# A two-block transformer: the first loads in another order, x's first chunk ahead of the first weight splits, and buffers in multiples of 32 columns

## The chip, the core and the metric

The kernel runs on one core of a Trainium2 chip. The core has a matrix engine (TensorE, PE in the profile), a vector engine (VectorE, DVE), a scalar engine for functions by table (ScalarE, ACT), a general engine (GpSimd, POOL) and an engine that only issues transfers (SyncE, SP). ScalarE and GpSimd can issue transfers too, and 16 DMA engines carry them out. The metric is the time of one execution on the device in microseconds (us), as the median of several runs.

## The reference

Two transformer blocks follow each other on one sequence of 256 tokens of width 2048, all in float32. The weights are drawn at random; the large ones are read once each.

```
h = layer_norm(a*x + hybrid_mixer(x))          # block 1
h = layer_norm(a*h + memory_cross_attention(h, mem))
h = layer_norm(a*h + conv_ffn(h))
for layer in (0, 1):                           # block 2
    n = rmsnorm(h)
    h = h + (even_mixer(n) if layer == 0 else short_conv(n))
    h = h + mlp(rmsnorm(h))                    # relu squared, 2048 -> 8192 -> 2048
```

The hybrid mixer multiplies x by one wide matrix `w_in` and cuts the product into pieces for three mixers, whose outputs stand side by side before `w_out`:

- S5: a diagonal complex recurrence along the tokens. Its coefficients come from small tables (exponential, cosine, sine and a division of the parameters), and the recurrence is a scan.
- Stick-breaking attention (SB): 8 heads of 64 with a running sum of logarithms in place of the softmax.
- Sparse attention (NSA): 16 heads of 64 with a compressed branch, a selected branch and a window. For the compressed branch, blocks of 32 keys (and values) get a position added and go through a small two-layer network, whose first weights are `nsa_cmp_w1`.

The even mixer of block 2 has attention heads with low-rank keys and values and an average over windows of tokens.

## The kernel before, in words

**Weights.** Nearly all the time is products of 256 tokens with large weights. The weights come in chunks of 1 MB (512 rows by 512 columns) on SyncE's queue (`load`, L628) into a ring of three buffers `raw`. Each float32 product is made of three products of a faster number type: a chunk is split into a high part `whi`, made by ScalarE (`split_hi`, L645), and the rest `wlo`, made by VectorE (`split_lo`, L655), each in two halves of 128 x 1024 and in rings of four. The activations are split likewise into slots `rt`. One half is used by four weight groups of TensorE: two matmuls of 512 columns and two of 256, or three of 512. A chunk's buffer is free again when its second half is split, and a half's when TensorE has used it.

**Order.** Nothing is reordered on the chip: each engine works through a list that is fixed when the program is built, and semaphores hold an instruction until its operands are there. The list is written by a planner, the `Builder`. It walks through the weight groups one by one. Beside them it has "side threads", generators that issue everything else in small steps: the transposes of x, S5's set-up and its chunks, the heads of the attentions, the sums of the compressed branch. After each group `advance` (L509) takes steps from the side threads as long as its own clocks of the engines allow. These clocks are estimates: `spent` (L438) adds one for each instruction, and `region` (L423) remembers, for each stretch of 32 columns of a buffer, when it was last written and last read. `wait_for` (L544) takes steps until something that is needed is there. The space for buffers is given out by an `Arena`; among the holes that are large enough it prefers one whose stretches are free soonest (`late`, L123). A step of a thread is thus put elsewhere when an estimate, the size of a buffer or its place changes.

**Start.** `network` (L2939 to L2963) issues the first loads: `load_consts` (L800) the constants `cbig` (128 x 1004, with the unit matrix `ident` in its first 128 columns) on ScalarE's queue; then, for each of four chunks c, `stage` (L2526) a quarter of x (512 KB; the first on SyncE's queue, the other three on ScalarE's) and, for the first three, a weight chunk on SyncE's queue. At c = 2 GpSimd makes a copy of one column that reads x's third chunk; GpSimd's own loads, some 20 small ones, stand behind it. `s5.load`, `nsa.load` and `load_cols` (L819) issue the small parameters. `run` (L752) first splits two halves (`ahead(2)`, L755), then goes through the plan; at the start of the first entry `start` (L2564) queues the side threads: S5's set-up and, for each chunk of x, `trans` (L2531), which transposes four pieces of 128 columns on TensorE, two matmuls each, and splits them into `rt`.

**Places the rows speak of.** h0 and h1 are the first products of the compressed branch, for keys and for values: 16 matmuls of 128 x 60 each, written by `hid_part` (L2604), which read `nsa_cmp_w1` from `raw` and the blocks that `NSA.gather` (L2287) has collected and added the positions to (an addition of 128 x 960). S5's set-up (`S5.setup`, L1895) runs on GpSimd, VectorE, ScalarE and, with small matmuls of 33 rows, on TensorE; `S5.chunk` (L2060) is one piece of the scan. Nearly every instruction has the line of the recording helper, L233, so rows are told apart by operation and buffers: `ft` is the space for float32 buffers, `st` a small one, `bank` a bank of the matmul's accumulators.

## Time and profile before

| | |
|---|---|
| median of 3 runs | 3513.49 us (3511.28 to 3513.76) |
| the profiled execution | 3515.05 us |
| its span in the trace | 3513.3 us, so 1.75 us lie around it |
| mean granted clock of TensorE | 0.989 of full speed |
| TensorE busy | 3426.3 us, 98% of the span |
| VectorE busy | 2371.4 us, 67% |
| ScalarE busy | 1725.5 us, 49% |
| GpSimd busy | 215.7 us, 6% |
| moved by the DMA engines | 605.15 MB, 172 GB/s on the mean |

A row of the timeline gives the start and the duration of an instruction, or of several alike that follow each other (x and a count), and in brackets how long the engine stood idle before it and what ended that. Float32 matmuls and matmuls of two passes appear as two records each. A row of a table of stretches gives, for each engine, its busy time and in parentheses its number of records. The granted clock is the share of full speed that the chip allows TensorE: 1.00 is 2.4 GHz and 0.50 is 1.2 GHz; a figure in between is a mean over a stretch. The chain that ended last is TensorE's work for 87% of the span and VectorE's for 10%.

### The profile page before, as it was taken

What the parts mean: (1) busy time and instruction counts of PE and PEld (TensorE: products, weight loads), DVE (VectorE), ACT (ScalarE), POOL (GpSimd) and SP (SyncE); (2) the same over time, 40 slices, a digit from 0 to 9 for tenths busy, and PEclk for the clock granted to TensorE, in tenths of its full rate; (3) what the DMA queues carried; (4) which work ended last, traced back from release to release, by engine and by line L of the source; (5) the groups of instructions that cost most, each with busy time, mean ns of one, the idle gap of its engine ahead of it and who ended that gap; (6) DMA issues with size and microseconds to landing.
All of it is one profiled execution on the core that took longest, in us unless ns stands there. A gap on an engine that the chain in (4) does not pass through costs nothing.

```text
span 3513.3 us, 49562 instructions
## 1 busy us (share of the span) xinstructions
PE 3426.3 (98%) x19448; PEld 2940.8 (84%) x19448; DVE 2371.4 (67%) x3978; ACT 1725.5 (49%) x2652; POOL 215.7 (6%) x319
## 2 busy tenths in 40 slices
PE   8998999899999999999999999999999999999999
PEld 6777688788888887787888888888888888888887
DVE  4977677876676578877765656567666664656565
ACT  4445645555455455654544444444454544434343
POOL 4001010001000001000000000000221000000001
PEclk8999999999999999999999999999999999999999
DMA  5452244355555555443555555555555555555554
GB/s 181 132 166 96 56 168 165 134 192 188 187 191 192 187 186 167 150 126 126 170 190 192 188 186 189 192 180 192 184 189 191 192 191 186 187 191 192 186 187 143
DMA packets 323779, 605.15 MB, mean 172 GB/s; under 512 B 18843, under 2 KB 36243, under 8 KB 323545
## 3 DMA queue, kind: packets, MB, share of 16 engines
q1 hardware_dynamic: 319609, 596.91, 51.5%
q10 hardware_dynamic: 3264, 4.19, 0.5%
q8 instruction: 152, 2.49, 0.3%
q0 software_dynamic: 672, 0.89, 0.1%
q14 instruction: 82, 0.67, 0.1%
HBM read 599.26 MB, written 2.69 MB: 171 GB/s over the span
## 4 chain that ended last, share of the span: by engine, by line
PE 87%; DVE 10%; issue 1%; ACT 1%; POOL 1%; DMA 1%; ACTq 0%; SPq 0%; DVEq 0%; POOLq 0%
PE bank L233 87%; DVE ft L233 6%; DVE wlo L233 3%; POOL ft L233 1%; DVE rt L233 0%; ACT ft L233 0%; DMA ft<-in_x_dram 0%; ACT whi L233 0%; DMA raw<-in_w_in_dram 0%; DMA raw<-in_even_w_ukv_dram 0%; DMA raw<-in_even_w_uq_dram 0%; POOL st L233 0%; DVE st L233 0%; ACT rt L233 0%; ACT L284 0%
## 5 line engine op out<-in xcount | busy, mean ns | idle before, releaser
L233 PE MATMUL bank<-rt,whi 128*128 128x512 f32 (+1 forms) x8784 | 2785.7, 399 | 47.6 <-DVE ft L233 27.3
L233 PEld LDWEIGHTS bank<-rt,wlo 128*128 128x128 f32 (+1 forms) x8784 | 1651.7, 189 | 388.8 <-DVE wlo L233 0.4
L233 DVE TENSOR_TENSOR wlo<-raw,whi 128x1024 fp32r<-128x1024 f32 x1134 | 1379.2, 1222 | 719.6 <-ACT whi L233 717.1
L233 ACT ACTIVATE whi<-raw 128x1024 fp32r<-128x1024 f32 x1134 | 1189.4, 1050 | 1344.3 <-PE bank L233 1271.5
L233 PE MATMUL bank<-rt,wlo 128*128 128x256 f32 (+1 forms) x8784 | 1727.8, 279 | 0.0
L233 PEld LDWEIGHTS bank<-rt,whi 128*128 128x128 f32 (+1 forms) x8784 | 1347.6, 189 | 79.6 <-DVE ft L233 28.9
L233 DVE TENSOR_TENSOR ft<-bank,ft 128x256 f32<-128x256 f32 (+2 forms) x879 | 358.3, 420 | 286.7 <-ACT ft L233 198.5
L233 POOL TENSOR_TENSOR ft<-ft 128x256 f32<-128x256 f32 (+1 forms) x179 | 149.1, 844 | 2912.8 <-DVE ft L233 2061.4
L233 ACT ACTIVATE ft<-bank 128x256 f32<-128x256 f32 (+3 forms) x499 | 190.4, 392 | 189.7 <-PE bank L233 161.1
L233 PE MATMUL bank<-ft 128*128 128x128 f32 (+9 forms) x1073 | 213.5, 346 | 33.9 <-DVE ft L233 21.8
L233 DVE SCALAR_TENSOR_TENSOR ft<-ft 128x256 f32<-128x256 f32 (+2 forms) x441 | 225.8, 513 | 13.0 <-ACT ft L233 2.5
L233 PEld LDWEIGHTS bank<-ft 128*128 128x128 f32 (+4 forms) x1073 | 137.6, 171 | 87.6 <-DVE ft L233 25.4
L233 ACT ACTIVATE ft<-ft 128x256 f32<-128x256 f32 (+3 forms) x365 | 165.8, 467 | 90.4 <-DVE ft L233 70.1
L233 DVE TENSOR_TENSOR ft<-ft 128x256 f32<-128x256 f32 (+4 forms) x463 | 194.1, 442 | 14.1 <-ACT ft L233 8.7
L233 ACT ACTIVATE rt<-ft 128x256 fp32r<-128x256 f32 x317 | 138.6, 439 | 85.2 <-DVE ft L233 80.3
L233 DVE TENSOR_TENSOR rt<-ft,rt 128x256 fp32r<-128x256 f32 x220 | 91.7, 445 | 5.2 <-ACT rt L233 5.2
L233 PE MATMUL bank<-whi,rt 128*128 128x256 f32 (+1 forms) x320 | 80.6, 329 | 1.4 <-DVE ft L233 1.4
L233 ACT ACTIVATE ft<-ft,st 128x256 f32<-128x256 f32 (+1 forms) x146 | 64.5, 464 | 19.3 <-DVE st L233 18.5
L233 PEld LDWEIGHTS bank<-whi,rt 128*128 128x128 f32 x320 | 55.5, 190 | 7.6 <-ACT whi L233 1.2
L233 PE MATMUL bank<-wlo,rt 128*128 128x256 f32 (+1 forms) x160 | 52.1, 326 | 0.0
L233 DVE SCALAR_TENSOR_TENSOR rt<-ft,rt 128x256 fp32r<-128x256 f32 x97 | 45.1, 475 | 0.3 <-ACT rt L233 0.3
L233 ACT ACTIVATE rt<-bank 128x256 fp32r<-128x256 f32 x56 | 20.0, 380 | 45.0 <-PE bank L233 44.9
(76 smaller groups left out, 464.9 us busy)
## 6 DMA issues: line engine op xcount, KB each, us to landing
raw<-in_w_mlp_up_dram SPq DMA_DIRECT2D x128, 1024.0 KB, 5.3
raw<-in_w_mlp_down_dram SPq DMA_DIRECT2D x128, 1024.0 KB, 5.1
raw<-in_ffn_w_up_dram SPq DMA_DIRECT2D x88, 1024.0 KB, 5.0
raw<-in_odd_w_in_dram SPq DMA_DIRECT2D x48, 1024.0 KB, 5.2
raw<-in_ffn_w_down_dram SPq DMA_DIRECT2D x44, 1024.0 KB, 5.1
raw<-in_w_in_dram SPq DMA_DIRECT2D x36, 1024.0 KB, 5.1
raw<-in_w_out_dram SPq DMA_DIRECT2D x16, 1024.0 KB, 5.1
raw<-in_even_w_in_dram SPq DMA_DIRECT2D x16, 1024.0 KB, 5.4
```

The lines of the kernel that those rows point to most:

```text
L233: return f(*a, **kw)
```

## The change

Four things are changed. The call that splits the first two halves moves from `run` into `start`, behind the whole transposition of x's first chunk (`now` runs a side thread to its end); the other three chunks of x are side threads as before. Only the 128 columns of the unit matrix are loaded first on ScalarE's queue; the other 876 columns of `cbig` come on SyncE's queue behind the third weight chunk. All of x comes on SyncE's queue, so that this queue has, in order: x's first chunk, a weight chunk, x's second, a weight chunk, x's third, a weight chunk, the rest of `cbig`, x's last chunk, then the small parameters. And three buffers are rounded up: `cbig` from 1004 to 1024 columns, the parameter columns from 584 to 608, the buffer of GpSimd's copy from 1 to 32. With that every buffer in `ft` begins at a multiple of 32 columns.

```diff
--- before.py
+++ after.py
@@ -752,7 +752,6 @@
     def run(self):
         self.halves = [(i, j) for i, e in enumerate(self.plan) for j in range(e.nhalf)]
         self.nhi = self.nlo = self.nhalf = 0
-        self.ahead(2)
         for i, e in enumerate(self.plan):
             for f in e.before:
                 f()
@@ -799,8 +798,9 @@
 
     def load_consts(self):
         nc = self.nc
-        self.cb = self.buf(CBIG.shape[1], True)
-        nc.scalar.dma_start(out=self.cb.ap, in_=self.I["cbig"])
+        self.cb = self.buf(1024, True)
+
+        nc.scalar.dma_start(out=self.cb.ap[:, 0:128], in_=self.I["cbig"][:, 0:128])
         nc.vector.tensor_copy(out=self.identr, in_=self.cst("ident"))
         self.ones = self.buf(128, True)
         nc.vector.memset(self.ones.ap, 1.0)
@@ -819,7 +819,7 @@
     def load_cols(self):
 
         nc = self.nc
-        self.pcol = self.buf(NCOL, True)
+        self.pcol = self.buf((NCOL + 31) // 32 * 32, True)
         nt = (NCOL + 127) // 128
         st = self.buf(nt * 128)
         sv = st.v(nt)
@@ -2525,7 +2525,7 @@
 
     def stage(n, c):
         stg[n, c] = B.buf(1024)
-        (nc.scalar if n == "x" and c else nc.sync).dma_start(out=stg[n, c].v(2), in_=I[n][0, :, c * 512:(c + 1) * 512].rearrange("(t p) f -> p t f", p=128))
+        nc.sync.dma_start(out=stg[n, c].v(2), in_=I[n][0, :, c * 512:(c + 1) * 512].rearrange("(t p) f -> p t f", p=128))
         return stg[n, c]
 
     def trans(n, c, lin=False):
@@ -2562,8 +2562,10 @@
     RT = 0.9
 
     def start():
+        now(trans("x", 0))
+        B.ahead(2)
         B.side(s5.setup())
-        for c in range(4):
+        for c in range(1, 4):
             B.side(trans("x", c), B.ready(stg["x", c].ap))
         B.side(B.turn_cols(), 40000.0)
         B.side(nsa.setup(), 45000.0)
@@ -2950,9 +2952,10 @@
         if c < B.NRAW:
             B.load(c)
         if c == 2:
-
-            t = B.buf(1)
-            nc.gpsimd.tensor_copy(out=t.ap, in_=x.ap[:, 0:1])
+            nc.sync.dma_start(out=B.cb.ap[:, 128:CBIG.shape[1]], in_=I["cbig"][:, 128:])
+
+            t = B.buf(32)
+            nc.gpsimd.tensor_copy(out=t.ap[:, 0:1], in_=x.ap[:, 0:1])
     s5.load()
     nsa.load()
     B.load_cols()
```

The planner's list differs from the first instructions on. The number of instructions hardly does: TensorE has 18896 in both, VectorE 3982 for 3980, ScalarE 2582 for 2586 with 25 loads of function tables for 22 (five scalings went from ScalarE to VectorE), GpSimd 326 for 324. Three places show how the order changes.

The first is TensorE's list at its beginning: before it was this, with transposes of x (`bank<-ft`, 128x128, two to a piece), the transpose of a small 48-row buffer, and the groups of the first weight chunk (`whi0`, `whi1`, and `wlo` of the same number); semaphores with DMAHW stand for loads.

```order
L233 MATMUL bank4_84<-ft_78 128x128 [waits DMAHW1_49,DMAHW0_49]
...
L233 MATMUL bank5_85<-ft_78 128x128 [waits DMAHW2_49]
...
L233 MATMUL bank6_86<-ft_78 128x48 [waits DMASW1_49,DMASW0_49,DVE_49]
L233 MATMUL bank7_87<-ft_78 128x128 x2
L233 MATMUL bank4_84<-ft_78 128x128 [waits DVE_49]
...
L233 MATMUL bank5_85<-ft_78 128x128 [waits DMAHW4_49,DVE_49]
...
L233 MATMUL bank3_83<-rt_76,whi0_68 128x512 [waits Activation_49]
L233 MATMUL bank3_83<-rt_76,whi0_68 128x512 [waits DVE_49]
L233 MATMUL bank3_83<-rt_76,wlo0_72 128x256 x2
...
L233 MATMUL bank7_87<-ft_78 128x128 [waits DMAHW5_49]
...
L233 MATMUL bank2_82<-rt_76,whi0_68 128x512 x2
...
L233 MATMUL bank3_83<-rt_76,whi1_69 128x512 [waits Activation_49]
```

Now the list begins like this:

```order
L233 MATMUL bank4_84<-ft_78 128x128 [waits DMAHW1_49,DMAHW0_49]
...
L233 MATMUL bank5_85<-ft_78 128x128 x2
L233 MATMUL bank6_86<-ft_78 128x128 x2
L233 MATMUL bank7_87<-ft_78 128x128 x2
L233 MATMUL bank3_83<-rt_76,whi0_68 128x512 [waits DVE_49,Activation_49]
L233 MATMUL bank3_83<-rt_76,whi0_68 128x512 [waits DVE_49]
...
L233 MATMUL bank2_82<-rt_76,whi0_68 128x512 x2
...
L233 MATMUL bank3_83<-rt_76,whi1_69 128x512 [waits Activation_49]
...
L233 MATMUL bank4_84<-ft_78 128x128 [waits DMAHW3_49]
...
L233 MATMUL bank5_85<-ft_78 128x128 [waits DMAHW5_49]
...
L233 MATMUL bank7_87<-ft_78 128x128 [waits DMAHW0_49]
...
L233 MATMUL bank3_83<-rt_76,whi2_70 128x512 [waits Activation_49]
```

x's first chunk is transposed whole, all eight groups of the first weight chunk follow, and only then come x's second, third and last chunk (the waits for DMAHW3, DMAHW5 and DMAHW0) and the first group of the second weight chunk (`whi2`).

The second place is where h0 (`raw_67`) and h1 (`raw_65`) stand. On TensorE they were neighbours, between the groups of two weight chunks:

```order
L233 MATMUL bank_81<-whi_69,rt 128x512
L233 MATMUL bank_80<-ft,raw_67 128x60 x16
L233 MATMUL bank_83<-ft,raw_65 128x60 x16
L233 MATMUL bank_82<-rt,whi_70 128x512 x2
L233 MATMUL bank_82<-rt,wlo_74 128x256 x2
```

On VectorE the stretch around them was this, from the split of the halves 59 and 60 (`wlo_74`, `wlo_75`) to those of the next chunks:

```order
L233 TENSOR_TENSOR wlo2_74<-raw1_66,whi2_70 128x1024
L233 TENSOR_TENSOR wlo3_75<-raw1_66,whi3_71 128x1024
L233 SCALAR_TENSOR_TENSOR ft_78<-ft_78 128x256
L233 TENSOR_TENSOR ft_78<-ft_78 128x256
L233 MEMSET ft_78 128x128 x2
L233 TENSOR_TENSOR wlo0_72<-raw2_67,whi0_68 128x1024
L233 TENSOR_TENSOR wlo1_73<-raw2_67,whi1_69 128x1024
L233 TENSOR_TENSOR wlo2_74<-raw0_65,whi2_70 128x1024
```

Now TensorE has 25 small matmuls between h0 and h1, of S5's chunks (32x256, 128x256) and of the attention heads:

```order
L233 MATMUL bank_81<-whi_69,rt 128x512
L233 MATMUL bank_80<-ft,raw_67 128x60 x16
L233 MATMUL bank_87<-ft 32x256 x2
L233 MATMUL bank_85<-ft 128x256 x2
...
L233 MATMUL bank_84<-ft 32x256 x4
L233 MATMUL bank_87<-ft 128x256 x2
...
L233 MATMUL bank_85<-ft 128x256
...
L233 MATMUL bank_85<-ft 128x256
L233 MATMUL bank_85<-ft 128x128 x2
L233 MATMUL bank_83<-ft,raw_65 128x60 x16
L233 MATMUL bank_82<-rt,whi_70 128x512 x2
```

And VectorE has 67 instructions between the same split and the next one (shown are some of them; the two of 128x960 are the gather's additions, for h0 and for h1):

```order
L233 TENSOR_TENSOR wlo2_74<-raw1_66,whi2_70 128x1024
L233 TENSOR_TENSOR wlo3_75<-raw1_66,whi3_71 128x1024
L233 TENSOR_TENSOR ft_78<-ft_78 128x256 x3
...
L233 TENSOR_TENSOR ft_78<-ft_78,st_79 128x960
...
L233 TENSOR_TENSOR ft_78<-ft_78 128x256 x5
...
L233 TENSOR_TENSOR ft_78<-bank5_85,ft_78 128x256 x2
...
L233 SCALAR_TENSOR_TENSOR ft_78<-ft_78 128x256
...
L233 COPY ft_78<-ft_78 64x16x15
...
L233 SCALAR_TENSOR_TENSOR ft_78<-bank6_86,ft_78 128x384
L233 TENSOR_TENSOR ft_78<-ft_78,st_79 128x960
...
L233 TENSOR_TENSOR wlo0_72<-raw2_67,whi0_68 128x1024
```

A block of S5's scan, of the heads and of the second gather, which stood between later splits and behind them, now stands between the two splits, and h0 waits for its first addition of 960 columns, h1 for its second.

The third place is in the even mixer of block 2, where the first of its heads' matmuls (`bank<-ft`, 128x256) come on TensorE. Before:

```order
L233 MATMUL bank_80<-rt,whi_70 128x512 x2
L233 MATMUL bank_80<-rt,wlo_74 128x256 x2
...
L233 MATMUL bank_83<-rt,whi_71 128x512 x2
L233 MATMUL bank_83<-rt,wlo_75 128x256 x2
L233 MATMUL bank_87<-ft 128x256
L233 MATMUL bank_86<-ft 128x256
L233 MATMUL bank_85<-ft 128x256
L233 MATMUL bank_84<-ft 128x256
```

Now:

```order
L233 MATMUL bank_81<-rt,whi_70 128x512 x2
L233 MATMUL bank_81<-rt,wlo_74 128x256 x2
L233 MATMUL bank_86<-ft 128x256
L233 MATMUL bank_80<-rt,whi_70 128x512 x2
L233 MATMUL bank_80<-rt,wlo_74 128x256 x2
L233 MATMUL bank_83<-rt,whi_70 128x512 x2
L233 MATMUL bank_83<-rt,wlo_74 128x256 x2
L233 MATMUL bank_84<-ft 128x256
```

The first of these matmuls stands six weight groups earlier, and they are spread between the groups. From TensorE's row 1400 on, this place and the last 200 rows are where the two lists differ in more than the names of buffers and pairs of neighbours.

## Rows read from the trace of the kernel before

**Rows 1.** the page's busy time: engine, busy us and share, instructions

```profile
PE 3426.3 (98%) x19448; PEld 2940.8 (84%) x19448; DVE 2371.4 (67%) x3978; ACT 1725.5 (49%) x2652; POOL 215.7 (6%) x319
```

**Rows 2.** waits of TensorE in the whole program: us, times, longest us

```profile
PE bank L233 <- DVE ft L233: 51.0, 49, 5.9
...
PE bank L233 <- DMA ft<-in_x_dram: 9.1, 2, 6.7
```

**Rows 3.** stretches: busy us (records) of each engine, granted clock, DMA, GB/s

```profile
40.00:60.00 20.00, 18.52 (x77) 16.34 (x75) 9.59 (x22) 5.78 (x13) 11.62 (x36) 0.60 0.30 91
200.00:220.00 20.00, 19.04 (x108) 15.30 (x108) 19.62 (x40) 9.17 (x15) 0.00 (x0) 1.00 0.51 172
308.00:320.00 12.00, 11.19 (x41) 8.33 (x38) 6.05 (x15) 8.73 (x19) 3.04 (x10) 0.50 0.17 43
348.00:354.00 6.00, 5.54 (x20) 4.99 (x21) 3.17 (x12) 5.94 (x11) 2.23 (x5) 0.50 0.01 3
1550.00:1600.00 50.00, 45.57 (x270) 39.44 (x270) 29.29 (x79) 27.14 (x61) 0.00 (x0) 0.93 0.35 116
1800.00:1850.00 50.00, 50.00 (x289) 43.62 (x288) 29.09 (x38) 24.09 (x35) 0.00 (x0) 1.00 0.55 189
```

**Rows 4.** timeline of the start: start us, us, engine, operation [wait, releaser]

```profile
6.74 0.66 PE L233 MATMUL bank<-ft 128*128 128x128 f32 x2 [6.74 <-DMA ft<-in_x_dram]
...
11.84 2.00 ACT L233 ACTIVATE whi<-raw 128x1024 fp32r<-128x1024 f32 x2 [7.15 <-DMA raw<-in_w_in_dram]
12.43 0.19 POOL L233 COPY st<-ft 128x1 f32<-128x1 f32 x1 [9.45 <-DMA ft<-in_x_dram]
...
17.23 0.77 PE L233 MATMUL bank<-rt,whi 128*128 128x512 f32 x1
```

**Rows 5.** stretches in the loading phase, columns as before

```profile
18.00:24.00 6.00, 4.90 (x27) 4.23 (x25) 3.99 (x8) 4.08 (x9) 5.00 (x13) 1.00 1.11 172
29.00:36.00 7.00, 7.00 (x41) 6.11 (x41) 3.98 (x4) 2.50 (x3) 5.95 (x16) 1.00 1.05 397
```

**Rows 6.** timeline of S5's set-up, VectorE and TensorE

```profile
42.63 0.21 DVE L233 COPY ft<-st 33x128 f32<-33x128 f32 x1
...
42.90 0.91 PE L233 MATMUL bank<-ft 33*128 33x383 f32 x2 [1.48 <-DVE ft L233]
...
66.09 0.18 DVE L233 COPY st<-bank 128x32 f32<-128x32 f32 x1
```

**Rows 7.** timeline around h0 and h1, ScalarE, VectorE, TensorE

```profile
240.36 2.01 ACT L233 ACTIVATE whi<-raw 128x1024 fp32r<-128x1024 f32 x2 [3.61 <-DMA raw<-in_w_in_dram]
...
241.46 2.36 DVE L233 TENSOR_TENSOR wlo<-raw,whi 128x1024 fp32r<-128x1024 f32 x2 [5.04 <-ACT whi L233]
...
243.65 7.25 PE L233 MATMUL bank<-ft,raw 128*128 128x60 f32 x64
```

**Rows 8.** VectorE's groups by form, 100 to 303 us: busy us, mean ns

```profile
L233 DVE TENSOR_TENSOR wlo<-raw,whi 128x1024 fp32r<-128x1024 f32 x55 | 67.5, 1230 | 16.2 <-ACT whi L233 16.2
L233 DVE TENSOR_TENSOR ft<-ft 128x256 f32<-128x256 f32 x114 | 46.5, 433 | 1.9
L233 DVE TENSOR_TENSOR ft<-bank,ft 128x256 f32<-128x256 f32 x62 | 23.3, 415 | 2.7 <-PE bank L233 2.7
L233 DVE TENSOR_TENSOR_SCAN ft<-ft 128x256 f32<-128x256 f32 x28 | 19.5, 697 | 0.0
...
L233 DVE TENSOR_TENSOR ft<-ft,st 128x960 f32<-128x960 f32 x2 | 2.3, 1148 | 0.0
```

**Rows 9.** timeline of TensorE where the mixer of block 1 runs out

```profile
307.80 7.40 PE L233 MATMUL bank<-ft 128*32 128x256 f32 x28 [3.84 <-DVE ft L233]
...
348.46 4.53 PE L233 MATMUL bank<-ft 128*128 128x128 f32 x16 [5.87 <-DVE ft L233]
```

**Rows 10.** timeline of TensorE behind the heads of block 2

```profile
1578.23 0.47 PE L233 MATMUL bank<-rt,whi 128*128 128x512 f32 x1 [1.74 <-DVE ft L233]
...
1580.88 1.19 PE L233 MATMUL bank<-rt,whi 128*128 128x512 f32 x2 [1.36 <-DVE ft L233]
```

## The prediction

> **What bounds the kernel now.** I read the page's busy shares first: TensorE is busy in 3426.3 of 3513.3 us [rows 1]. So a change in the order of the work can give or take only from some 87 us of idle time and from the time that the clock stands low. The reader is to see next what TensorE waits for: nearly all is VectorE's buffers, 51.0 us in 49 waits; x's transfer costs 9.1 us [rows 2]. Then the table of stretches [rows 3]: at 1800 to 1850 us 289 matmul records stand in 50 us at full clock and nothing is to be had (a weight group is four of them, 0.69 us); what a new order can touch lies at 40 to 60 us (granted clock 0.60), 308 to 320 (0.50), 348 to 354 (0.50) and 1550 to 1600 (0.93, TensorE busy 45.57 of 50). At 0.50 the clock is at the lower of its two levels, 1.2 GHz. The same table shows the second thing that matters: VectorE is busy 19.62 of 20 us at 200 to 220. There VectorE, not TensorE, sets the pace, and a TensorE that comes early only waits.
>
> **Part one, the start.** Before, x's first chunk comes together with the whole of cbig, the first transpose runs at 6.74, the first weight chunk can be split only at 11.84, and the first weight matmul starts at 17.23 [rows 4]. In the new order x's chunk and 64 KB of cbig come first, 576 KB instead of 1014 KB ahead of the first transpose: I put that at 5.2 us (between 4.5 and 6.74). The first weight chunk is next on the queue: 1 MB at the 397 GB/s that one queue moved at 29 to 36 us [rows 5] is 2.6 us, so it lands at 7.8; split, and the first weight matmul starts at about 9.2 (between 8.5 and 17.23). That is 8 us early. All eight groups of that chunk can run before x's second chunk.
>
> What of the 8 us arrives? Two things eat it. First, S5's set-up. Its chain on GpSimd starts behind x's third chunk, 12.43 before [rows 4]; now 3.67 MB stand up to it on one queue, at 397 GB/s 9.2 us behind a first byte at 3.7 (5.2 less 1.5 for the first 0.59 MB), so 12.9: 0.5 us late. In the old order VectorE's copy that releases the 33-row matmul comes at 42.63 and that matmul at 42.90 [rows 6]. VectorE's new order puts ahead of the same copy four additions from PSUM (0.376 each) and a second pass of five table operations (0.408 each, the nearest row) [rows 8]; the one weight split there stood there before. That is 1.5 + 2.0 = 3.5 us, with GpSimd's 0.5 together 4.0: 42.9 + 4.0 = 46.9. TensorE comes to it with some seven groups (7 x 0.69 = 4.9 us) more behind it, so here 4.9 - 4.0 = 0.9 us of the 8 are left as work done; the rest became a wait. Second, the stretch in which VectorE has no slack [rows 3]: it begins with S5's tables, behind the copy at 66.09 [rows 6], and gets no more out of an early TensorE than that 0.9. So the start gives +1 us: between -4 (x's last chunk, now last of the big loads, holds the second weight chunk's matmuls, see the rivals) and +5 (all of the seven groups arrive).
>
> **Part two, the two matmul groups h0 and h1 of the compressed branch.** This is the largest term, and it comes not from the loads but from the buffers: with sizes that are multiples of 32 columns the planner's regions no longer overlap, and it writes another order. Before, h0 and h1 are adjacent and take 7.25 us at 243.65 without a wait. VectorE finishes the two splits that stand before them at 243.8, since the weight chunk for it landed only at 240.36 [rows 7]. In the new order 67 VectorE instructions stand between those splits and the next one (five chunks of S5's scan, pieces of the attention, two additions of 960 columns), h0 waits for the first of the two additions and h1 for the second. What they cost, from VectorE's own rows at 100 to 303 us [rows 8]: 33 additions from SBUF at 46.5/114 = 0.408 are 13.5; 12 from PSUM at 23.3/62 = 0.376 are 4.5; 7 scans at 0.697 are 4.9; the two wide additions at 1.148 are 2.3; the other 13, small ones, at the 0.408 of the nearest row, 5.3. Sum 30.5 us. The block cannot begin earlier than those splits, which hang on the same chunk as before; so it begins when TensorE arrives at h0. In the 30.5 us TensorE has h0 (7.25/2 = 3.6) and 25 small matmuls of two records each; 28 such records took 7.40 us at half clock [rows 3, 9], so 50 take 13.2 at half and are worth 6.6 at full clock. Lost are 30.5 - 3.6 - 6.6 = 20.3 us, some 14 to 20 of them seen as idle time. After a wait of 5.87 the clock stood at half for 6 us of work [rows 3, 9], which costs 3.0: in all -23 us. Bounds: -12, if VectorE comes to the block while TensorE still has half a chunk's matmuls; -30, if none of the small matmuls fits between and the clock is slow to return.
>
> What comes back: the same VectorE work is then not needed at 303 to 354 us, where TensorE before waits 3.84 and 5.87 and runs 12 + 6 us at half clock [rows 3, 9]: 9.7 + 6.0 + 3.0 = 18.7 us. In the new order the compressed branch and the attention's heads are spread over the groups ahead of that place, and only eight small matmuls are left there. I take 18.7 as returned, and 2 us for waits between the spread pieces (0 to 8), since single groups of 0.69 us stand between them. Together 18.7 - 2 - 23 = -6 us (between -18 and +7).
>
> The Trainium skill, "TensorE: Matmul & The Clock Gate", Part 1, says that "the default state is throttled, and activity releases the throttle". By it, sparse small matmuls inside a long wait need not hold the clock up; the 28 records from 307.80, at 0.50, agree [rows 3, 9]. It speaks against splitting h0 from h1; with h1 itself at half clock the term would be 3.6 us worse.
>
> **Part three, block 2's first mixer.** Its heads start six weight groups earlier on TensorE. Two of the waits behind them, 1.74 and 1.36 us [rows 10], and part of the clock's loss of 0.07 x 50 = 3.5 us there [rows 3] may go: +2 us, between -4 and +8 (nothing in the rows says that the order there is better by itself).
>
> **The rest at nothing.** Three more table loads on ScalarE and five scalings moved to VectorE lie beside work of TensorE; a wide addition of VectorE's, 1.148 us, is the nearest row to each, so uncovered the eight cost 9 us, which I keep in the range.
>
> **Sum.** +1 - 6 + 2 = -3, so the profiled execution goes from 3515.05 (span 3513.3 and 1.75 around it) to 3518; the median of the runs shown, 3513.49, lies 1.6 lower, so I forecast 3517.
>
> **Rivals.** *The early start is kept* (faster). If VectorE's early splits carry through the full stretch, the start gives 5; VectorE then comes to the block at h1 some 7 us before TensorE does, -16 instead of -23, and the return is the full 18.7; with +3 in block 2: 5 - 16 + 18.7 + 3 = +10.7, 3503. For it: the split of a half takes VectorE 1.23 us [rows 8], and those made early fall out of the stretch without slack. Against it: the split ahead of h0 hangs on a chunk that can't be issued sooner [rows 7]. *The block is paid and not returned* (slower). The waits at 303 and 348 us end last on chains (scan, softmax through ScalarE and VectorE), not on VectorE's load. If a chain of that length stands in the new place too, only the first half returns, 3.84 + 6.0 = 9.8: 1 - 23 - 2 + 9.8 + 2 = -12, 3526. It decides as soon as less than 11 of the 18.7 come back. For it: the two waits were ended by VectorE right behind such chains. Against it: the spread pieces lie well ahead of their readers. *x's last chunk is late.* Before, the third weight chunk took from 15.2 to 22.3 us, while GpSimd's small loads ran, at 172 GB/s over 18 to 24 us against 397 later [rows 5]. x's last chunk now has that place, and TensorE needs it before the second weight chunk: if that chunk, with the third weight chunk and cbig's rest 2.03 MB behind 12.9, moves at 172 GB/s, it lands at 24.7, and not at about 21 as I put it (between 18.0 at 397 GB/s and this): the start -3 instead of +1, 3521. The Trainium skill, "DMA: Bandwidth & Descriptors", "Queues, rings and completion order", has each DMA engine take packets in turn from the queues that have work, so one queue does not keep GpSimd's loads out; its section "Issuing engines are not separate DMA queues" says the same of the gain: order changes, bandwidth does not. *The order doesn't matter*: VectorE's block overlaps TensorE's matmuls, nothing is lost at h1 and nothing gained later, 3513.
>
> **Chances.** Forecast 0.37, kept start 0.24, block not returned 0.24, late chunk 0.08, no change 0.07. 0.2% is 7 us, about what a measurement of this kernel tells from no change: faster means below 3506.5, slower above 3520.5. The forecast's own range is 3510 to 3524. Faster: the kept start and a little of the forecast, 0.27; slower: the unreturned block, a quarter of the forecast and a third of the late chunk, 0.35; within: 0.38. The range of 8 in 10 reaches to both outer cases: 3500 to 3530.
>
> **What would show it.** In the changed profile: the first weight matmul near 9 us and the 33-row matmul near 47; if that stays at 43, the start is worth more. Between h0 and h1 some 20 us of TensorE's idle time, ended by VectorE, and half clock behind it; if h1 follows within 10 us, part two is wrong. No wait above 2 us in the two places that answer to 307.80 and 348.46. The waits at 1578 and 1580 gone. A wait of TensorE on x's transfer until 24 us would speak for the late chunk.

## The result and the profile after

The changed kernel takes 3549.66 us (median, 3549.3 to 3554.29), the kernel before 3513.62 us (3511.28 to 3515.06) beside it: a ratio of 1.0107, 95% interval 1.0094 to 1.0119. It is 36 us slower, where 3517 with a range up to 3530 was forecast.

First the page's head and busy time of the changed kernel, which answer to [rows 1]:

```profile
span 3548.2 us, 49522 instructions
...
PE 3442.5 (97%) x19448; PEld 2951.4 (83%) x19448; DVE 2377.5 (67%) x3980; ACT 1736.0 (49%) x2651; POOL 222.4 (6%) x321
```

The span is 34.9 us longer, and TensorE is "busy" 16.2 us longer with the same 19448 records. So some of the loss is idle time and some is the same work at a lower clock. What TensorE waits for (us in all, times, longest us), as in [rows 2]:

```profile
PE bank L233 <- DVE ft L233: 58.6, 49, 7.7
PE bank L233 <- DVE rt L233: 26.6, 10, 6.4
PE bank L233 <- DMA ft<-in_x_dram: 5.7, 1, 5.7
PE bank L233 <- ACT ft L233: 4.5, 6, 2.3
```

The waits for VectorE grew from 51.0 to 58.6 us on the buffers `ft` and from 19.8 to 26.6 on the slots `rt`, which the prediction did not count when it put nearly all of the waiting at 51.0; the wait for x shrank from 9.1 to 5.7. None of these names a place. The table of stretches does, with the columns of [rows 3]:

```profile
40.00:60.00 20.00, 15.05 (x59) 12.47 (x59) 11.34 (x29) 6.79 (x16) 12.25 (x47) 0.63 0.21 67
200.00:220.00 20.00, 17.00 (x86) 12.36 (x86) 19.43 (x43) 7.92 (x15) 2.39 (x4) 0.91 0.41 144
245.00:295.00 50.00, 34.15 (x120) 23.35 (x119) 29.88 (x71) 16.96 (x28) 1.99 (x4) 0.55 0.12 42
295.00:345.00 50.00, 49.94 (x361) 43.39 (x360) 28.95 (x60) 27.68 (x53) 12.70 (x32) 0.97 0.35 114
...
370.00:395.00 25.00, 16.05 (x78) 11.49 (x78) 14.92 (x54) 18.02 (x40) 5.33 (x8) 0.80 0.28 86
390.00:395.00 5.00, 5.00 (x19) 3.49 (x19) 2.25 (x10) 2.89 (x8) 0.57 (x1) 0.68 0.18 26
...
1600.00:1650.00 50.00, 42.99 (x219) 33.53 (x218) 35.42 (x119) 30.40 (x76) 0.00 (x0) 0.93 0.37 127
```

At 245 to 295 us the granted clock is 0.55 and TensorE is busy 34.15 of 50 us; at 370 to 395 it is busy 16.05 of 25 at 0.80; at 1600 to 1650, 42.99 of 50 at 0.93. From 200 to 220 VectorE is as full as before (19.43 us for 19.62), but TensorE is busy 17.00 us at 0.91, where it was busy 19.04 at 1.00.

Where the time goes stage by stage can be counted by the weight matmuls: there are 18,048 records of them in either trace, in the same order, so that the start of the n-th can be compared.

| weight matmul record | what stands there | before, us | after, us | after less before |
|---|---|---|---|---|
| 1 | the first | 17.23 | 9.49 | -7.7 |
| 841 | some 12 us ahead of h0 | 230.95 | 232.70 | +1.7 |
| 1101 | behind h0, h1 and a part of the heads | 283.54 | 349.67 | +66.1 |
| 1581 | behind all of the hybrid mixer's heads | 484.54 | 512.03 | +27.5 |
| 2401 | block 1's FFN | 683.40 | 714.92 | +31.5 |
| 6901 | behind the first half of the even mixer | 1494.13 | 1525.75 | +31.6 |
| 7901 | block 2's MLP | 1729.26 | 1764.40 | +35.1 |
| 18048 | the last | 3506.78 | 3541.71 | +34.9 |

From record 841 to record 1581, 25.8 us are lost. The +66.1 at 1101 is not loss alone, since pieces of the heads come earlier than before. The layer norms and the cross-attention cost 4.0 (1581 to 2401), and 3.5 are lost from record 6901 to 7901, in block 2's first mixer and just behind it.

The start, as in [rows 4] and [rows 6] (start us, us, engine, operation, in brackets the idle time ahead and what ended it):

```profile
5.70 1.94 PE L233 MATMUL bank<-ft 128*128 128x128 f32 x8 [5.70 <-DMA ft<-in_x_dram]
...
8.38 2.00 ACT L233 ACTIVATE whi<-raw 128x1024 fp32r<-128x1024 f32 x2 [0.33 <-DMA raw<-in_w_in_dram]
...
9.49 1.22 PE L233 MATMUL bank<-rt,whi 128*128 128x512 f32 x2 [1.85 <-ACT whi L233]
...
13.82 0.99 POOL L233 COPY st<-ft 128x1 f32<-128x1 f32 x1 [10.83 <-DMA ft<-in_x_dram]
...
47.49 1.64 PE L233 MATMUL bank<-ft 33*128 33x383 f32 x2 [3.35 <-DVE ft L233]
```

The weight chunk is there at 8.38 for 11.84, the first weight matmul starts at 9.49 for 17.23, GpSimd's copy is at 13.82 for 12.43, and the 33-row matmul comes at 47.49 for 42.90, behind a wait of 3.35. Of the 7.7 us nothing is left at 231 us.

Around h0 and h1, where [rows 7] had both in 7.25 us, TensorE now:

```profile
249.84 7.08 PE L233 MATMUL bank<-ft,raw 128*128 128x60 f32 x32 [4.29 <-DVE ft L233]
256.85 5.78 PE L233 MATMUL bank<-ft 128*32 128x256 f32 x16
270.36 1.06 PE L233 MATMUL bank<-ft 128*32 128x256 f32 x2 [7.73 <-DVE ft L233]
272.03 6.50 PE L233 MATMUL bank<-ft 128*32 128x256 f32 x18 [0.62 <-DVE ft L233]
281.15 1.06 PE L233 MATMUL bank<-ft 128*32 128x256 f32 x2 [2.62 <-DVE ft L233]
282.81 4.64 PE L233 MATMUL bank<-ft 128*32 128x256 f32 x12 [0.59 <-DVE ft L233]
287.24 6.92 PE L233 MATMUL bank<-ft,raw 128*128 128x60 f32 x32
```

h0 waits 4.29 and takes 7.08 for 3.6; small matmuls follow with waits of 7.73 and 2.62; h1 comes 37.4 us behind h0 and takes 6.92. Over h0 and over h1 the granted clock is 0.50, the lower of the two levels (columns of [rows 3]):

```profile
249.84:256.92 7.08, 7.08 (x33) 6.97 (x34) 3.61 (x11) 1.28 (x1) 0.00 (x0) 0.50 0.15 58
287.24:294.16 6.92, 6.92 (x34) 6.92 (x34) 0.00 (x0) 2.39 (x4) 0.00 (x0) 0.50 0.01 2
```

And VectorE there:

```profile
246.57 1.09 DVE L233 TENSOR_TENSOR ft<-ft 128x256 f32<-128x256 f32 x3
...
258.80 0.48 DVE L233 SCALAR_TENSOR_TENSOR ft<-ft,bank 128x256 f32<-128x256 f32 x1 [5.18 <-PE bank L233]
260.80 0.76 DVE L233 TENSOR_TENSOR ft<-bank,ft 128x256 f32<-128x256 f32 x2 [1.52 <-PE bank L233]
...
275.20 0.76 DVE L233 TENSOR_TENSOR ft<-bank,ft 128x256 f32<-128x256 f32 x2 [2.62 <-PE bank L233]
...
283.49 1.15 DVE L233 TENSOR_TENSOR ft<-ft,st 128x960 f32<-128x960 f32 x1
```

The reader should look at the brackets of these rows: VectorE itself waits 5.18, 1.52 and 2.62 us for TensorE's small matmuls. The two engines take turns, each idle while the other works.

Where [rows 9] had its waits, TensorE has these now, at 370 to 395 us:

```profile
372.93 1.67 PE L233 MATMUL bank<-ft 64*128 64x128 f32 x8 [1.49 <-DVE st L233]
...
383.97 0.90 PE L233 MATMUL bank<-ft 128*128 128x128 f32 x3 [2.34 <-ACT ft L233]
389.50 1.33 PE L233 MATMUL bank<-rt,whi 128*128 128x512 f32 x2 [4.63 <-DVE rt L233]
```

And for [rows 10], in block 2:

```profile
1607.84 0.47 PE L233 MATMUL bank<-rt,whi 128*128 128x512 f32 x1 [1.31 <-DVE ft L233]
...
1616.76 1.19 PE L233 MATMUL bank<-rt,whi 128*128 128x512 f32 x2 [5.69 <-DVE ft L233]
```

Before, the two waits of [rows 10] had one more ahead of them:

```profile
1574.52 0.47 PE L233 MATMUL bank<-rt,whi 128*128 128x512 f32 x1 [1.32 <-DVE ft L233]
```

The waits of 1.32, 1.74 and 1.36 us there have become 1.31 and 5.69.

### The profile page after: what moved, and what is told of

Same layout as the page of the kernel before. It is cut to its first block, busy times and chain, and to the rows that moved or that the text cites. A ratio compares the mean times of both kernels' runs of the same rounds, so it can differ in the third digit from the quotient of the medians.

```text
span 3548.2 us, 49522 instructions
## 1 busy us (share of the span) xinstructions
PE 3442.5 (97%) x19448; PEld 2951.4 (83%) x19448; DVE 2377.5 (67%) x3980; ACT 1736.0 (49%) x2651; POOL 222.4 (6%) x321
## 4 chain that ended last, share of the span: by engine, by line
PE 87%; DVE 8%; ACT 1%; issue 1%; DMA 0%; SPq 0%; DVEq 0%; ACTq 0%
PE bank L233 87%; DVE ft L233 5%; DVE wlo L233 2%; ACT ft L233 1%; DVE rt L233 0%; ACT whi L233 0%; DMA raw<-in_even_w_out_dram 0%; DMA raw<-in_w_in_dram 0%; ACT L233 0%; ACT L284 0%; DMA raw<-in_even_w_uq_dram 0%; ACT rt L233 0%; SPq L233 0%; DVEq L233 0%; ACTq L233 0%
## 5 line engine op out<-in xcount | busy, mean ns | idle before, releaser
L233 DVE TENSOR_TENSOR ft<-bank,ft 128x256 f32<-128x256 f32 (+1 forms) x879 | 358.9, 420 | 264.8 <-ACT ft L233 178.8
L233 POOL TENSOR_TENSOR ft<-ft 128x256 f32<-128x256 f32 (+1 forms) x181 | 156.5, 877 | 2919.0 <-DVE ft L233 2064.7
L233 ACT ACTIVATE ft<-bank 128x256 f32<-128x256 f32 (+4 forms) x498 | 192.5, 391 | 177.8 <-PE bank L233 174.0
L233 PE MATMUL bank<-ft 128*128 128x128 f32 (+10 forms) x1073 | 218.6, 350 | 35.6 <-DVE ft L233 19.3
L233 PEld LDWEIGHTS bank<-ft 128*128 128x128 f32 (+5 forms) x1073 | 138.5, 171 | 93.7 <-DVE ft L233 24.8
L233 DVE TENSOR_TENSOR ft<-ft 128x256 f32<-128x256 f32 (+4 forms) x461 | 197.8, 452 | 15.9 <-ACT ft L233 10.5
L233 DVE CUSTOM_DVE_ANT_0 ft<-bank,ft 128x128 f32<-128x128 f32 x80 | 25.5, 355 | 18.4 <-PE bank L233 14.0
```

What stands on the lines that cost most here:

```text
L233: return f(*a, **kw)
```

## The experiments

Two theories stood against each other, and a third beside them. A: the rounded sizes made the planner write h1's gather late, and the wait for it is the loss. B: the loads are. C: any new order costs, here and there. Each experiment's edit is given against the kernel before or the changed kernel. The second column of the table gives the median and the ratio to the runs of the kernel before beside it. The others give how much later than in the kernel before the weight matmul records of the table above start, in us, from one profiled execution of each, which can be some us off the median. How far chance reaches is seen in before_ksl: TensorE's list in it is that of the kernel before up to 247 us, and yet it is 3.1 us ahead at record 841, since at 55 to 66 us the granted clock was 0.82 in it and 0.50 in the kernel before. So a difference of some 3 us at 841 says nothing.

| kernel | median us, ratio to before (95%) | at 841 | 1101 | 1581 | 2401 | 7901 |
|---|---|---|---|---|---|---|
| the change | 3549.66, 1.0107 (1.0094 to 1.0119) | +1.7 | +66.1 | +27.5 | +31.5 | +35.1 |
| start_only | 3523.42, 1.0032 (1.0021 to 1.0044) | -5.3 | -3.4 | +7.2 | +8.5 | +8.4 |
| early_only | 3523.22, 1.0028 (1.0018 to 1.0038) | -5.7 | -3.7 | +9.3 | +10.0 | +8.8 |
| loads_only | 3538.67, 1.0074 (1.0059 to 1.0089) | -9.5 | -6.5 | +25.0 | +27.2 | +24.6 |
| sizes_only | 3536.91, 1.0073 (1.0058 to 1.0088) | +4.7 | +60.8 | +14.1 | +16.3 | +19.2 |
| sizes_loads | 3535.85, 1.0068 (1.0052 to 1.0083) | +0.1 | +56.1 | +12.5 | +16.8 | +20.7 |
| gather_first | 3520.42, 1.0031 (1.0017 to 1.0045) | -3.5 | -1.2 | -1.5 | +2.3 | +5.0 |
| ksl_between | 3523.51, 1.0034 (1.0021 to 1.0046) | +0.6 | +23.7 | -1.6 | +2.6 | +6.6 |
| gather_first_ksl | 3511.35, 0.9998 (0.9989 to 1.0007) | -0.7 | +7.3 | -6.9 | -2.8 | +0.9 |
| filled_waits | 3558.86, 1.0132 (1.0118 to 1.0146) | +3.5 | +74.5 | +37.8 | +42.0 | +45.9 |
| before_ksl | 3506.84, 0.9983 (0.9974 to 0.9992) | -3.1 | +1.1 | -11.5 | -9.3 | -11.5 |
| loads_gather_ksl | 3500.47, 0.9959 (0.9946 to 0.9973) | -1.7 | +9.8 | -18.5 | -12.4 | -14.5 |
| before_gather_ksl | 3515.39, 1.0005 (0.9996 to 1.0014) | -1.8 | +8.0 | -5.6 | +0.6 | -0.6 |

**start_only: the change without the rounded sizes.**

```diff
-        self.cb = self.buf(1024, True)
+        self.cb = self.buf(CBIG.shape[1], True)
...
-        self.pcol = self.buf((NCOL + 31) // 32 * 32, True)
+        self.pcol = self.buf(NCOL, True)
...
-            t = B.buf(32)
-            nc.gpsimd.tensor_copy(out=t.ap[:, 0:1], in_=x.ap[:, 0:1])
+            t = B.buf(1)
+            nc.gpsimd.tensor_copy(out=t.ap, in_=x.ap[:, 0:1])
```

> The changed kernel with the three buffer sizes put back (1004, 584, 1): load order and x's early transposes alone; h0 and h1 stand side by side again in the written order. Theory A (the rounded sizes made the planner put S5's chunks between h0 and h1, and that is the loss): the 36 us go, 3513 us, between 3506 and 3520, no wait between h0 and h1; what remains against before is the start's own worth, +1 with -4 to +5. Rival B (the loss comes from the loads, above all x's last chunk and GpSimd's chain being late): 3535 or more. Rival C (any new order costs many small waits, wherever): 3525 to 3545, without one place that holds more than 10 us.

3523.42 us: 26 us go, but it is still 1.0032 times the kernel before beside it, some 11 us, and above the range that theory A gave. h0 and h1 are adjacent, and at record 1101 this kernel is 3.4 us ahead. The remaining loss, 10.6 us, falls between 283 and 484 us, at S5's gated product (weight records 1217 to 1248): the kernel is 4.5 us ahead at record 1216 and 9.5 behind at 1248.

**sizes_only: the kernel before with the three rounded sizes.**

```diff
-        self.cb = self.buf(CBIG.shape[1], True)
-        nc.scalar.dma_start(out=self.cb.ap, in_=self.I["cbig"])
+        self.cb = self.buf(1024, True)
+        nc.scalar.dma_start(out=self.cb.ap[:, 0:CBIG.shape[1]], in_=self.I["cbig"])
...
-        self.pcol = self.buf(NCOL, True)
+        self.pcol = self.buf((NCOL + 31) // 32 * 32, True)
...
-            t = B.buf(1)
-            nc.gpsimd.tensor_copy(out=t.ap, in_=x.ap[:, 0:1])
+            t = B.buf(32)
+            nc.gpsimd.tensor_copy(out=t.ap[:, 0:1], in_=x.ap[:, 0:1])
```

> The kernel before with nothing but the three rounded sizes (1024, 608, 32); h0 and h1 are split by 15 rows of small matmuls as in the changed kernel. Theory A: 3545 us, between 3535 and 3555, with some 40 us lost from h0 to the end of h1 and some 28 won back behind it. Rival B (loads): 3513. Rival C: slower too, but spread.

3536.91 us: slower, within theory A's range. TensorE between h0 and the end of h1 in it:

```profile
265.29 1.06 PE L233 MATMUL bank<-ft 128*32 128x256 f32 x2 [8.79 <-DVE ft L233]
...
276.07 1.06 PE L233 MATMUL bank<-ft 128*32 128x256 f32 x2 [2.62 <-DVE ft L233]
...
282.16 6.92 PE L233 MATMUL bank<-ft,raw 128*128 128x60 f32 x32
```

The waits of 8.79 and 2.62 us and h1 at half clock are those of the changed kernel, with the old loads and the old start. So the place is made by the sizes alone.

**gather_first: the changed kernel, the gathers at the head of the queue.**

```diff
-                B.side(nsa.gather(j // 2))
+                B.side(nsa.gather(j // 2), prio=0)
```

> The changed kernel with the two gather threads queued ahead of all other threads (priority 0 for 1), so that both get one of the planner's six places and h0 and h1 stand side by side; loads, early transposes and rounded sizes stay. Theory A: 3515 us, between 3505 and 3523. Rival C: stays above 3530, since the rounded sizes disturb the order elsewhere too. Rival B: stays near 3550.

3520.42 us, 29 us of the 36 are back. h0 and h1 stand in one row again:

```profile
242.40 7.25 PE L233 MATMUL bank<-ft,raw 128*128 128x60 f32 x64
```

The planner has six places for threads that have begun (`DEPTH = 6`). When the two gathers are queued, its own list shows four threads under way before the change and five after it, so one gather found no place, and `wait_for` at h1 wrote S5's chunks until one became free. With the priority nothing else was changed, so this mechanism is shown.

**loads_only: the kernel before with the new order of the loads.**

```diff
-        nc.scalar.dma_start(out=self.cb.ap, in_=self.I["cbig"])
+        nc.scalar.dma_start(out=self.cb.ap[:, 0:128], in_=self.I["cbig"][:, 0:128])
...
-        (nc.scalar if n == "x" and c else nc.sync).dma_start(out=stg[n, c].v(2), in_=I[n][0, :, c * 512:(c + 1) * 512].rearrange("(t p) f -> p t f", p=128))
+        nc.sync.dma_start(out=stg[n, c].v(2), in_=I[n][0, :, c * 512:(c + 1) * 512].rearrange("(t p) f -> p t f", p=128))
...
+            nc.sync.dma_start(out=B.cb.ap[:, 128:CBIG.shape[1]], in_=I["cbig"][:, 128:])
```

> The kernel before with only the order of the loads changed (the unit matrix first, the rest of cbig and all of x on one queue); x's first chunk is not put ahead of the first splits, sizes as before. Theory A: 3513 us, between 3507 and 3520. Rival B: 3530 or more, with a wait of TensorE on x's last chunk or on GpSimd's chain.

3538.67 us, where theory A said 3513. That is rival B's number, but not its place: the waits for x are 12.3 us in three (9.1 in two before), all of them at the start, and all the same the kernel is 9.5 us ahead at record 841. What it loses, it loses from 300 us on:

```profile
300.29 3.92 PE L233 MATMUL bank<-ft 128*32 128x256 f32 x8 [5.77 <-DVE ft L233]
309.43 3.91 PE L233 MATMUL bank<-ft 128*32 128x256 f32 x8 [5.22 <-DVE ft L233]
318.56 7.40 PE L233 MATMUL bank<-ft 128*32 128x256 f32 x26 [5.22 <-DVE ft L233]
329.63 10.61 PE L233 MATMUL bank<-ft 128*128 128x256 f32 x49 [3.67 <-POOL ft L233]
```

Here three chunks of S5 are written one behind the other ahead of S5's gated product, since `wait_for` finds them undone there. They come 9.1 us apart (309.43 - 300.29, 318.56 - 309.43), with 5.2 us of idle time in each. The kernel before has the first of such waits, 3.84 us [rows 9]. So theory A was too narrow: a loss is made wherever `wait_for` writes chunks in a row, and each start leaves another number of them.

**ksl_between: the changed kernel, a weight product between h0 and h1.**

```diff
-ORDER = "u5 sq sk kv nq0 nq1 g sv h0 h1 ksl units ksw"
+ORDER = "u5 sq sk kv nq0 nq1 g sv h0 ksl h1 units ksw"
```

> The changed kernel with one word of ORDER moved: the entry ksl (one 512-column weight product, 32 groups and some 29 us of TensorE) stands between h0 and h1 and no longer behind them; the gather of h1 and S5's chunks then lie beside its weight groups. Theory A (the loss is made while TensorE waits for h1, with small matmuls and VectorE taking turns at half clock): the 64 us between h0 and the end of h1 shrink by 25 to 40 and what comes later keeps its gain, 3549 to 3510, between 3495 and 3522. Rival C (the rounded sizes cost everywhere): 3535 or more.

3523.51 us, 26 us back, just above the range. TensorE at h0 and at h1:

```profile
246.49 5.21 PE L233 MATMUL bank<-ft,raw 128*128 128x60 f32 x32 [2.11 <-DVE ft L233]
...
289.18 3.68 PE L233 MATMUL bank<-ft,raw 128*128 128x60 f32 x32
```

42.7 us lie between the two, but 32 weight groups are in them, and h1 comes without a wait and at full clock (3.68).

**gather_first_ksl: the two edits together, with ksl ahead of h0.**

```diff
-ORDER = "u5 sq sk kv nq0 nq1 g sv h0 h1 ksl units ksw"
+ORDER = "u5 sq sk kv nq0 nq1 g sv ksl h0 h1 units ksw"
...
-                B.side(nsa.gather(j // 2))
+                B.side(nsa.gather(j // 2), prio=0)
```

> The changed kernel with the gathers queued first and ksl ahead of h0 and h1, so that no chunk of S5 is left either when h1 comes or when the gated product of S5 comes; in the planner's own list no wait for a gather or for S5 remains. Theory A, extended (every stretch in which wait_for writes S5's chunks one behind the other costs about 10 us a chunk, wherever it stands): faster than gather_first (3520), 3503, between 3493 and 3513. Against it: the S5 chunks were already cheap in gather_first, no gain, 3520.

3511.35 us, within the range of theory A extended and 9 us below gather_first; against the kernel before it is no difference (0.9989 to 1.0007). At record 1581 it is 6.9 us ahead, at 7901 0.9 behind: 4.1 us go in the norms and the cross-attention and 3.7 up to 7901. Every kernel with rounded sizes shows the second of these (+2.7 to +4.0 from 2401 to 7901), no kernel with the old sizes does (-2.6 to -0.1). The first is no mark of the sizes: from 1581 to 2401 kernels with the old sizes lose 0.7 to 6.2, those with the new 2.2 to 4.3.

**sizes_loads: the kernel before with the edits of sizes_only and of loads_only, both as they stand above.**

> The kernel before with the rounded sizes and the new order of the loads, without x's first chunk ahead of the splits; TensorE's written order is that of sizes_only, instruction by instruction, so that only the loads differ. Theory A: the loads are worth 0 to 9 us there (TensorE was 9.5 us ahead at h0 with the loads alone), 3532, between 3526 and 3540. Rival B (the loads cost): 3540 or more.

3535.85 us. With TensorE's order the same as in sizes_only the loads alone are worth 4.6 us at record 841 and nothing in the median (3536.91).

**early_only: x's first chunk ahead, with the old loads and sizes.**

```diff
-        self.ahead(2)
...
+        now(trans("x", 0))
+        B.ahead(2)
...
-        for c in range(4):
+        for c in range(1, 4):
```

> The kernel before with x's first chunk transposed and split ahead of the first weight splits, loads and sizes as before. Its written order is that of start_only but for the first groups and the banks. Theory A: some us slower than start_only (3523) since the first weight chunk lands later, 3526, between 3518 and 3535. Rival: early transposes are the part that costs, and the loads give some back; then 3530 or more.

3523.22 us, the same as start_only. It loses 13 us in the same stretch, between records 1101 and 1581.

**filled_waits: added work in the gaps.**

```diff
+    def filler(self, k):
+        if self.mixfree:
+            for _ in range(k):
+                self.nc.tensor._real.matmul(self.mixfree[0][:, 0:512], lhsT=self.ones.ap, rhs=self.cb.ap[:, 0:512], start=True, stop=True)
...
+        if B.fill:
+            B.filler(5)
         yield
...
+        def waits():
+            B.fill = j == 1
+            B.wait_for(lambda: j in nsa.G)
+            B.fill = False
+            if j == 0:
+                B.filler(6)
```

> The changed kernel with 16 added float32 matmuls of 512 columns (ones by constants) into a free bank, read by nobody: six ahead of h0, five behind each of two first matmuls of S5's chunks between h0 and h1; all other instructions and their order stay. If half of the price at h0 and h1 is the clock (h0 7.1 and h1 6.9 us at half clock for 3.6 at full, small matmuls that VectorE waits for at half speed), work in the gaps keeps the clock up and the kernel gets faster in spite of the added work: 3549 to 3538, between 3530 and 3545. If the price is VectorE's chain alone, the added matmuls only lie in the gaps or delay: 3549 to 3560.

3558.86 us, 9 slower, and in the range that was given for added matmuls that only lie in the gaps or delay. TensorE there (L350 is the added work):

```profile
247.16 5.31 PE L350 MATMUL bank<-ft 128*128 128x512 f32 x12
252.31 3.68 PE L233 MATMUL bank<-ft,raw 128*128 128x60 f32 x32
...
272.04 1.06 PE L233 MATMUL bank<-ft 128*32 128x256 f32 x2 [7.49 <-DVE ft L233]
...
293.64 6.92 PE L233 MATMUL bank<-ft,raw 128*128 128x60 f32 x32
```

Of VectorE's waits for TensorE behind h0:

```profile
257.00 0.48 DVE L233 SCALAR_TENSOR_TENSOR ft<-ft,bank 128x256 f32<-128x256 f32 x1 [1.41 <-PE bank L233]
...
263.61 0.76 DVE L233 TENSOR_TENSOR ft<-bank,ft 128x256 f32<-128x256 f32 x2 [4.33 <-PE bank L233]
```

And the two stretches:

```profile
240.00:260.00 20.00, 20.00 (x90) 13.82 (x89) 11.93 (x26) 7.10 (x10) 0.00 (x0) 1.00 0.46 151
260.00:280.00 20.00, 11.89 (x26) 4.82 (x25) 13.44 (x34) 0.00 (x0) 0.00 (x0) 0.69 0.02 7
```

h0 ran at full clock now, 3.68 us for 7.08. But h1 ended at 300.6 (293.64 + 6.92) against 294.2. Of these 6.4 us, 1.8 were lost ahead of record 841; the rest comes between. With h0 at full clock VectorE's first wait fell from 5.18 to 1.41, but behind the next five added matmuls it waited 4.33, TensorE's wait of 7.73 for VectorE is still 7.49, and h1 takes 6.92 as before. So added work in these places costs more than the clock gives back. How much of the price the clock has it does not show, since h1 and many of the small matmuls ran at half clock here too.

**before_ksl: the kernel before, ksl between h0 and h1.**

```diff
-ORDER = "u5 sq sk kv nq0 nq1 g sv h0 h1 ksl units ksw"
+ORDER = "u5 sq sk kv nq0 nq1 g sv h0 ksl h1 units ksw"
```

> The kernel before with only the entry ksl moved between h0 and h1. In its list no S5 chunk stands behind a wait any more (18 us of planned wait at S5's gated product before). Extended theory A: the waits of 3.84 us at 308 and the half clock behind it go, 3503, between 3495 and 3511. Rival: h1's gather is no problem here and the stretch is bound by VectorE either way, 3513.

3506.84 us, faster by 5.6 (0.9974 to 0.9992), in the range of theory A. The waits at 308 and 348 us are gone; at record 1581 it is 11.5 us ahead, 3.1 of them since before record 841.

**loads_gather_ksl: loads_only (its edit stands above) with the gathers first and ksl between; old sizes, x not ahead.**

```diff
-ORDER = "u5 sq sk kv nq0 nq1 g sv h0 h1 ksl units ksw"
+ORDER = "u5 sq sk kv nq0 nq1 g sv h0 ksl h1 units ksw"
...
-                B.side(nsa.gather(j // 2))
+                B.side(nsa.gather(j // 2), prio=0)
```

> The kernel before with the new order of the loads, the gathers queued first, and ksl between h0 and h1; x's first chunk not ahead, sizes not rounded. Extended theory A: the loads' lead at h0 (9.5 us in loads_only) stays, no chunk of S5 is written behind a wait, and the 3 + 4 us that all kernels with rounded sizes lost after 500 us are not paid: 3498, between 3488 and 3510. Rival: the lead is eaten in the stretch where VectorE has no slack, 3512.

3500.47 us, faster than both kernels (0.9946 to 0.9973 against the kernel before; of its five executions one, left out of the interval, took 10083 us, for which no cause is known). No wait stands at h0 or h1:

```profile
243.63 3.67 PE L233 MATMUL bank<-ft,raw 128*128 128x60 f32 x32
...
280.13 3.68 PE L233 MATMUL bank<-ft,raw 128*128 128x60 f32 x32
```

The lead did not come the way that was expected: at record 841 it is 1.7 us, and not 9.5. It is made between 1101 and 1581, 28 us of return for 12 paid up to 1101. And 6.1 us go again from 1581 to 2401, where the expectation had none.

**before_gather_ksl: the same two edits on the kernel before, with the old loads.**

```diff
-ORDER = "u5 sq sk kv nq0 nq1 g sv h0 h1 ksl units ksw"
+ORDER = "u5 sq sk kv nq0 nq1 g sv h0 ksl h1 units ksw"
...
-                B.side(nsa.gather(j // 2))
+                B.side(nsa.gather(j // 2), prio=0)
```

> loads_gather_ksl with the loads put back to those of the kernel before, so that only the gathers' priority and the place of ksl differ from it. If the gain of 12 us in loads_gather_ksl comes from the order of the side threads alone: 3503, between 3498 and 3508. If the loads carry their lead of some 4 to 9 us through the stretch in which VectorE has no slack: 3508 or more, 5 to 9 us above loads_gather_ksl.

3515.39 us, 15 above loads_gather_ksl, as the second case said, but again not for its reason. At record 841 the two are alike (-1.8 and -1.7). The difference comes behind them: from record 1101 to 1581 this kernel takes 187.4 us and loads_gather_ksl 172.7. TensorE is idle for 8.6 and 4.2 us of that, and the longest wait here stands at the first group of `w_out`, behind S5's gated product (record 1249):

```profile
357.00 0.79 PE L233 MATMUL bank<-rt,whi 128*128 128x512 f32 x1 [5.36 <-DVE rt L233]
```

The other 10 us of the difference are busy time of TensorE and were not traced. Together with sizes_loads, where the same list with the new loads was worth nothing in the median, this speaks for the loads working chiefly by the list that the planner writes, by way of its clocks, and not by when the data are there. It also says that the two edits alone bring nothing to the kernel before (0.9996 to 1.0014).

## Why the prediction was wrong, point by point

**The start** was forecast well in its steps: the first chunk at 7.8 (8.38), the first weight matmul at 9.2 (9.49), the 33-row matmul at 46.9 (47.49). Its worth was forecast at +1, between -4 and +5, and the changed kernel stands at -1.7 at record 841. That this lies inside the bounds is luck: start_only, with the same start and the old sizes, is 5.3 ahead there, early_only 5.7 and loads_only 9.5. So the stretch in which VectorE has no slack does not take the lead by itself, as was argued. With the rounded sizes put in, record 841 comes later by 4.7 us (sizes_only), 7.0 (the change against start_only) and 9.6 (sizes_loads against loads_only), and the prediction had no term for that; up to 1.7 us of it are small matmuls that one list has behind 841 and the other ahead, and what the rest is made of was not traced. The rival with x's last chunk at 24.7 fell: the first weight matmul behind that chunk's first transpose stands at 20.25, and the only wait for x ends at 5.70.

**The term of h0 and h1 failed**, and with it the forecast: a loss of 6 us was said for the whole of it, 25.8 is what the table shows. Its mechanism stands (sizes_only, gather_first); two sizes in it were wrong.

The first is the price, 23. TensorE could begin h0 at 245.55 (249.84 - 4.29), and ended h1 at 294.16: 48.6 us for work that was counted at 3.6 + 3.6 + 6.6 = 13.8 at full clock. So 34.8 were lost. The sum of VectorE's instructions, 30.5, was nearly right: it ran from 246.57 to 284.64, of which 9.3 us are the three waits in its rows, which leaves 28.8. The step that failed is the one that laid TensorE's small matmuls beside VectorE's block as if the two were independent. S5's chunk goes from TensorE to VectorE and back, so the block took VectorE's time and in addition TensorE's matmuls at half clock in between, and h0 and h1 at half clock, of which 3.0 us were charged. Against the forecast of 23 the end is 11.5 later: 9.3 are VectorE's waits for TensorE, 2.6 the matmuls that stand between VectorE's last addition and h1 (284.64 to 287.24), the rest cancels. A size was wrong with it: the small matmuls took 19.0 us at half clock (5.78 + 1.06 + 6.50 + 1.06 + 4.64), not 13.2; the row of 28 records in 7.40 us that they were counted from is a mixture of other forms. Seen from TensorE, 15.9 of the 34.8 us are idle time (4.29 + 7.73 + 0.62 + 2.62 + 0.59), inside the 14 to 20 that were forecast; the other 19 are work that was counted at less than its time at half clock. The Trainium skill, "TensorE: Matmul & The Clock Gate", Part 1, says that the throttled state is the default and that activity lifts it. The trace agrees: h0 took 7.08 us at 0.50 behind an idle gap of 4.29, and 3.68 behind the added matmuls of filled_waits. What this whole stretch would have taken at full clock no run here shows, so the clock's share of the price stays open.

The second is the return, 18.7 less 2. Between h1's end and record 1581, 34.8 - 25.8 = 9.0 came back. The waits of 3.84 and 5.87 are gone, but at 370 to 395 us TensorE stands idle 25 - 16.05 = 9.0 us, and at 390 to 395 it works at 0.68, which costs another 0.32 x 5 = 1.6. These are the same two places: the wait of 1.49 stands ahead of S5's gated product (records 1217 to 1248), those of 2.34 and 4.63 behind it, ahead of the first group of `w_out` (1249), which needs what VectorE makes of that product. The rival "the block is paid and not returned" came nearest here, with 9.8 returned, and went to 3526 only because it took the price of 23 from the forecast.

**Block 2's first mixer** was put at +2, between -4 and +8, because heads begin earlier. Up to record 7901, 3.5 us were lost: 1.3 by record 7451, behind the heads, where waits of 1.31 and 5.69 stand in place of three that add up to 4.4, and 2.2 behind it. The experiments put the 3.5 to the rounded sizes. What the 2.2 are made of was not traced.

**Missing from the list**: the norms and the cross-attention, 4.0 us, which the order showed only as moved transposes; and that the two other parts of the change write another list too, which costs 11 us in start_only and 26 in loads_only (by their ratios). These costs do not add up: the parts that cost 26, 10 and 26 alone (loads_only, early_only, sizes_only) cost 36 together. The rounding as such was taken to be neutral for the planner's quality. What makes the exact regions worse for the later stages is open: it was not tried apart from the sizes as a whole.

## What to carry to other kernels

Where a planner writes the order, a change of sizes or loads is first of all a new list: compare where its waits stand before anything is added up. A wait that writes leftover work of another thread costs that work's whole chain (here 9.1 us a chunk of S5), not the busy time of its slowest engine, since engines that take turns don't overlap. What helped was to give the needed thread its place early and to put dense independent work between the two consumers: each brought the changed kernel 26 to 29 us, and both together took the early loads, which alone were 9.5 us ahead at 231 us and ended 24.6 behind, to 12 us under the kernel before (3500.47 us, 0.9946 to 0.9973). It is no rule for every list: on the kernel before itself the two edits together brought nothing (3515.39 us), one of them alone 5.6 us (3506.84).

## What was not expected of the hardware

Twelve records of added float32 matmuls, 5.31 us in a gap that was idle before, kept the granted clock at 1.00 over 240 to 260 us, and h0 behind them took 3.68 us for 7.08. In the changed kernel one queue carried x, the weights and cbig's rest without a wait of TensorE for x behind the first chunk; loads_only waited 3.20 us for x's last chunk with the same queue.
